# Attention queries in one DRAM tensor, head by head, instead of plain and rotary rows in two

## The chip, the cores and the metric

The kernel runs on one core of a Trainium2 chip, as one launch. The metric is the device time in microseconds (us). The core has TensorE (PE, matrix products into PSUM; its weight loads are shown as PEld), VectorE (DVE), ScalarE (ACT), GpSimd (POOL), and SyncE (SP), which in this kernel issues all DMA transfers, in the order of its own instruction stream. A transfer is carried out by up to sixteen DMA engines, which move its rows as packets and then report its completion.

## The reference, cut to what matters

One encoder layer over 1024 positions with 1024 channels: multi-head latent attention and a bidirectional RWKV-7 mixing side by side, merged through gates, then a gated feed-forward part. What the change touches is the query of the attention, 8 heads of 64 plain and 32 rotary dimensions:

```python
q = (c_q @ w_uq).reshape(B, S, MLA_HEADS, QK_NOPE + QK_ROPE)          # 8 heads x (64 + 32)
q_nope, q_rope = q[..., :QK_NOPE], q[..., QK_NOPE:]
q_nope = rms_norm(q_nope, qn_g)
q_rope = rope(rms_norm(q_rope, qr_g), cos[:, :, None, :], sin[:, :, None, :])
...
def rope(t, cos, sin):                       # pairs (i, i + 16)
    half = t.shape[-1] // 2
    t1, t2 = t[..., :half], t[..., half:]
    return jnp.concatenate([t1 * cos - t2 * sin, t2 * cos + t1 * sin], axis=-1)
...
s = q_nope . k_nope + q_rope . k_rope        # one rotary key for all heads
p = softmax(s / sqrt(96));  o = p @ v
```

A score is a sum over 96 dimensions, and the order of these does not matter as long as query and key have the same.

## The kernel before, in words

All values are float32. Products that need precision are made of three: each operand is split into a high part, rounded to TensorE's fast format (`hi`), and the rest (`lo`), and hi*hi, hi*lo and lo*hi are summed in PSUM. So queries and keys exist twice, as high and low part. Channels lie on the partitions, positions along the free dimension, mostly in halves of 512 (`HT`).

The stages in order of time: the norm of x and the first columns of the input projection (to about 100 us); the rest of the projection (`inproj`), between whose matmuls the up-projections of the latents are strewn (to about 320 us); from then the chunked RWKV scans, between whose steps "dense" work is put (`gates`, the last columns of the projection; `attention`, from about 580 to 1000 us; `branch0`); then the merge and the feed-forward part. PE's order is written out by hand: generators yield pieces of work with their cost in ns, and a planner with modelled times of the other engines picks which comes next. The other engines' orders are made by the scheduler of the language. SP works through its stream one by one: a transfer that waits for its source holds up those behind it.

The weights of a projection tile come in halves of 512 columns (`wload`, line 219): a transfer into one of two `wraw` buffers, a copy on ACT to `whi`, a subtraction on POOL (or DVE) to `wlo`, each with two buffers. The load after next is issued when the subtraction has freed its `wraw`.

The queries are made in two kinds of pieces.

- `mla_nope(j, True)` (line 596), j = 0 to 3, two halves each: 128 rows, which are the 64 plain dimensions of heads 2j and 2j + 1. They are lifted out of PSUM, normed, split into `hi` and `lo` (two buffers each, tags `hi` and `lo`), and each is written by one transfer to 128 rows of `d_qh` or `d_ql` (512 rows of 1024 positions).
- `mla_rope` (line 640), two halves: the tiles hold 16 rows of each of the 8 heads, one tile for the first and one for the second half of the rotation (`out` = 0, 1). They go to `d_qrh` or `d_qrl`, which have the shape [128, 2, 1024]: row 16 * head + frequency, and within it the half. So a head's 32 rotary rows are contiguous, in the order frequency, half.

The rotary key (`key_rope`, line 545) is written to every second row of `d_krh` and `d_krl` to match that order.

In attention, two sets `qh`, `kh` of high parts alternate over the heads, and there is one set `ql`, `kl` of low parts. Rows 0 to 63 are plain, 64 to 95 rotary, the rest padding: row 96 of `qh` takes the negative row maximum of the scores (from `mr`, line 1307), and the rows of the rotary key and the padding are loaded once (`pad`). `load_h(h + 1)` (lines 1272 to 1274) is issued early in head h, `load_l(h + 1, part)` (lines 1278 to 1280) in the second half of head h, when the columns are free. `maxima(h + 1)` runs `sc<-kh,qh` matmuls within head h, as soon as `qh` is there.

Of the kernel before, what the change touches and what calls it, by code (L numbers as in the profile page):

```python
# [10 lines left out]
F32 = mybir.dt.float32  # L11
# [9 lines left out]
T = 1024  # L21
# [66 lines left out]
def block_kernel(ctx: ExitStack, tc: tile.TileContext, a):  # L88
    nc = tc.nc
# [94 lines left out]
    def vc(name, i=0, rows=slice(0, 128)):  # L184
        o = VOFF[name] + i
        return vec[rows, o:o + 1]

    def dt(name, shape):
        return dr.tile(shape, F32, name=name)
# [2 lines left out]
    d_gl = [dt(f"d_gl{d}", [128, T]) for d in range(2)]  # L192
    d_rw = {q: dt(f"d_{q}", [128, NPAIR, T]) for q in ("r", "v", "kk", "x1", "x2", "s0", "s1", "bo")}
    d_obf = dt("d_obf", [128, NPAIR, T])
    d_qh, d_ql = (dt(f"d_q{x}", [512, T]) for x in "hl")
    d_qrh, d_qrl = (dt(f"d_qr{x}", [128, 2, T]) for x in "hl")
    d_kh, d_kl = (dt(f"d_k{x}", [512, T]) for x in "hl")
    d_krh = dt("d_krh", [64, T])
    d_krl = dt("d_krl", [64, T])
# [10 lines left out]
    def split(x, hi, lo, eng=None):  # L210
        S.copy(hi, x)
        (eng or G).tensor_tensor(out=lo, in0=x, in1=hi.bitcast(F32), op=sub)
# [3 lines left out]
    def wload(src, n, tag="w", bufs=None):  # L216
        wp = wpool[tag]
        raw = wp.tile([128, n], F32, tag=f"{tag}raw", name=f"{tag}raw")
        wpool["load"] = nc.sync.dma_start(raw, src)
        hi = wp.tile([128, n], R, tag=f"{tag}hi", name=f"{tag}hi", bufs=bufs)  # L220
        lo = wp.tile([128, n], R, tag=f"{tag}lo", name=f"{tag}lo", bufs=bufs)
        split(raw, hi, lo)
        return hi, lo
# [18 lines left out]
    def rsqrt_(out, ss, scale, bias):  # L242
        act(out, ss, AF.Ln, scale=scale, bias=bias)
        act(out, out, AF.Exp, scale=-0.5)
# [47 lines left out]
    def up1():  # L292
        return psm.tile([128, 512], F32, tag="up", name="up")

    def ss1():
        return psm.tile([128, 512], F32, tag="ss", name="ss")
# [79 lines left out]
    def tt(n, tag="tp", bufs=3, dtype=F32, w=T):  # L376
        return tp.tile([128, w], dtype, tag=tag, name=n, bufs=bufs)
# [44 lines left out]
    for dst, src in ((b64r, a["consts"][:, C_B64:]), (b16, a["b16"])):  # L422
        t = tt("bt", "sqb", 1, w=128)
# [46 lines left out]
    def parted(x, hi=None, lo=None):  # L470

        if hi is None:
            hi, lo = t5("ghi", "ghi", GB, R), t5("glo", "glo", GB, R)
        S.copy(hi, x)
        V.tensor_tensor(out=lo, in0=x, in1=hi.bitcast(F32), op=sub)
        return hi, lo
# [13 lines left out]
    def mul(ps, w, x, **kw):  # L490
        now[0] += 213 if w.dtype == R else 853
        return E.matmul(ps, w, x, **kw)
# [28 lines left out]
    def key_rope():  # L521
        kro = slice(64, 128)
        sq = tt("sqk")
        S.activation(sq[kro, :], l2[kro, :], AF.Square)
        yield "kr"
        rs = tt("rsk")
        for hs in HT:
            ss = ss1()
            mul(ss[kro], onef[kro, 0:64], sq[kro, hs], start=True, stop=True)
            rsqrt_(rs[kro, hs], ss[kro], 1.0 / 32, eps[kro])  # L530
        kr = tt("kr")
        V.scalar_tensor_tensor(out=kr[kro, :], in0=l2[kro, :], scalar=vc("gkr", 0, kro), in1=rs[kro, :], op0=mult, op1=mult)
        yield "kr2"
        A_, B_ = slice(64, 96), slice(96, 128)
        ka, kb = sq, rs
        V.tensor_tensor(out=ka[kro, :], in0=kr[kro, :], in1=cosT[kro, :], op=mult)
        V.scalar_tensor_tensor(out=kb[A_, :], in0=kr[B_, :], scalar=-1.0, in1=sinT[B_, :], op0=mult, op1=mult)
        V.tensor_tensor(out=kb[B_, :], in0=kr[A_, :], in1=sinT[A_, :], op=mult)
        V.tensor_tensor(out=ka[kro, :], in0=ka[kro, :], in1=kb[kro, :], op=add)
        for hs in HT:  # L540
            hi, lo = t5("hi", "hi", HB, R), t5("lo", "lo", HB, R)
            split(ka[kro, hs], hi[kro], lo[kro], V)
            for dst, src in ((d_krh, hi), (d_krl, lo)):
                for half in range(2):
                    nc.sync.dma_start(dst[half:32:2, hs], src[64 + 32 * half:80 + 32 * half, :].bitcast(F32))
        yield "kr3"

        z = tt("z")
        G.memset(z[0:64, :], 0.0)
        G.memset(z[32:33, :], 1.0)  # L550
        for dst, src in ((d_zero, z[0:32, :]), (d_krl[32:64, :], z[0:32, :]), (d_krh[32:64, :], z[32:64, :])):
            nc.sync.dma_start(dst, src)
        yield "kr3"

    def up(ps, wh, wl, xs, hs):
        n = len(xs)
        for k, (xh, xl) in enumerate(xs):
            ws = slice(k * 128, (k + 1) * 128)
            mul(ps, wh[:, ws], xh[:, hs], start=(k == 0), stop=False)
            mul(ps, wh[:, ws], xl[:, hs], start=False, stop=False)  # L560
            mul(ps, wl[:, ws], xh[:, hs], start=False, stop=(k == n - 1))
# [4 lines left out]
    def t5(n, tag="hs", bufs=HS_BUFS, dtype=F32):  # L566
        return tt(n, tag, bufs, dtype, w=512)

    def lift(ps):
        q, sq = t5("q"), t5("sqh")  # L570
        S.activation(sq, ps, AF.Square)
        V.tensor_copy(q, ps)
        return q, sq
# [6 lines left out]
    def mla_nope(j, isq):  # L580
        xs, src, g = ((cqx, "w_uq", gqs[:, 0:1]), (ckx, "w_uk", vc("gkn")))[0 if isq else 1]
        w = []

        def half(hs):
            if not w:
                w.extend(wload(a[src][j], 128 * len(xs), "s"))
            ps = up1()
            up(ps, *w, xs, hs)
            q, sq = lift(ps)
            pt = parted(sq)  # L590
            yield "up"
            hnorm(sq, pt, b64r, 64.0, [q], [g])
            hi, lo = t5("hi", "hi", HB, R), t5("lo", "lo", HB, R)
            split(q, hi, lo, V)
            for qd, kd, x in ((d_qh, d_kh, hi), (d_ql, d_kl, lo)):
                nc.sync.dma_start((qd if isq else kd)[j * 128:(j + 1) * 128, hs], x.bitcast(F32))
        return [half(hs) for hs in HT]

    def staged(todo):
# [14 lines left out]
    def mla_rope():  # L614
        ws = []

        def half(hs):
            two = []
            if not ws:
                ws.extend(wload(a["w_uq"][4 + i], 256, "s") for i in range(2))  # L620
            for i in range(2):
                ps = up1()
                up(ps, *ws[i], cqx, hs)
                two.append(lift(ps))
                if i == 0:
                    yield "rope"
            (q1, s1), (q2, s2) = two
            G.tensor_tensor(out=s1, in0=s1, in1=s2, op=add)
            pt = parted(s1)
            yield "up"  # L630
            hnorm(s1, pt, b16, 32.0, [q1, q2], [gqs[:, 1:2], gqs[:, 2:3]])
            for out, op in enumerate((sub, add)):
                hi, lo = t5("hi", "hi", HB, R), t5("lo", "lo", HB, R)
                t, o = t5("t", "ht", 2), t5("o", "ht", 2)
                V.tensor_tensor(out=o, in0=two[out][0], in1=cosT[:, hs], op=mult)
                G.tensor_tensor(out=t, in0=two[1 - out][0], in1=sinT[:, hs], op=mult)
                V.tensor_tensor(out=o, in0=o, in1=t, op=op)
                split(o, hi, lo, V)
                for dst, src in ((d_qrh, hi), (d_qrl, lo)):
                    nc.sync.dma_start(dst[:, out, hs], src.bitcast(F32))  # L640
                if out == 0:
                    yield "rope3"
        return [half(hs) for hs in HT]
# [602 lines left out]
    ql = kl = vh = vl = None  # L1246
# [23 lines left out]
    def load_h(h):  # L1270
        qh, kh = qk[h % 2]
        nc.sync.dma_start(kh[0:64, :].bitcast(F32), d_kh[64 * h:64 * h + 64])
        nc.sync.dma_start(qh[0:64, :].bitcast(F32), d_qh[64 * h:64 * h + 64])
        nc.sync.dma_start(qh[64:96, :].bitcast(F32), d_qrh[16 * h:16 * h + 16].rearrange("i f t -> (i f) t"))

    def load_l(h, part):
        hs = HT[part]
        nc.sync.dma_start(ql[0:64, hs].bitcast(F32), d_ql[64 * h:64 * h + 64, hs])
        nc.sync.dma_start(ql[64:96, hs].bitcast(F32), d_qrl[16 * h:16 * h + 16].rearrange("i f t -> (i f) t")[:, hs])
        nc.sync.dma_start(kl[0:64, hs].bitcast(F32), d_kl[64 * h:64 * h + 64, hs])  # L1280

    def load_v(p, part):
# [355 lines left out]
    for u in range(NU):  # L1638
        osb = None if u else wk.tile([128, 2, 512], F32, tag="osb", name="osb")
        ch = chain(u, qs_[u], lambda: osb)  # L1640
        for k in range(9):
            want = [(u, None, "t"), (u, 0, "bt")] if k == 0 else [(u, 1, "bt")] if k == 3 else []
            sparse = 0
            while True:
                t = max([ready] + [seen.get(x, math.inf) for x in want])
# [4 lines left out]
                x = prepare(not blocked and (thin or sparse and t < math.inf), not blocked and 0 < alone[0] < BATCH and due > -math.inf)  # L1650
# [10 lines left out]
            x = next(ch, None)  # L1661
# [370 lines left out]
    x = load_next(2)  # L2032
# [38 lines left out]
    for f in range(2, NF):  # L2071
# [31 lines left out]
        else:  # L2103
            x = load_next(f + 1)
# [160 lines left out]
```

## Time and profile before

| | |
|---|---|
| median of the runs shown | 1877.03 us (1876.88 to 1881.24) |
| the profiled execution | 1880.9 us; its span on the core 1879.1 us |
| granted TensorE clock, mean | 0.981 |
| busy: PE, PEld, DVE, ACT, POOL | 1811.9, 1466.9, 1234.6, 872.6, 576.1 us |
| DMA | 260777 packets, 211.01 MB, nearly all on the queue q1, which SP feeds |
| plain queries written | 16 transfers of 256 KB (`d_qh`, `d_ql`), 254.9 to 316.1 us |
| rotary queries written | 8 transfers of 256 KB (`d_qrh`, `d_qrl`), 225.7 to 254.4 us |
| queries read | 8 + 8 transfers for the high part, 16 + 16 for the low part, 313.1 to 962.9 us |

The page of the profile gives, in order: each engine's busy time; the span in forty slices, with a digit for the busy tenths of each engine, of the DMA engines and of the granted clock; the DMA queues; the chain of work that ended last; the costliest groups of instructions; the DMA issues by group. In a row such as `L596 SPq DMA_DIRECT2D d_qh<-hi`, L596 is the line of the kernel, SPq the sequencer that issues, and `out<-in` are the program's names. A time in brackets behind an instruction is how long its engine stood before it, and whose end released it. Many operations are recorded at a helper's line (L109, L124), so that they are told apart by their tiles.

### The profile page before, as it was taken

The numbers are of one execution on the slowest core, as the hardware profiler recorded it, in microseconds if no ns is written. First come the engines' busy times: TensorE is split into PE (matmuls) and PEld (weight loads), VectorE is DVE, ScalarE is ACT, GpSimd is POOL, SyncE is SP. The second block draws the span as 40 slices with busy tenths as digits, with TensorE's granted clock in tenths as the row PEclk, the third lists the DMA queues.
The fourth block names the chain that finished last, engine by engine and source line by source line (L and its number), as shares of the span: only waits on it lengthen the run. The fifth ranks groups of instructions, "written<-read, shape, count | busy, mean of one in ns | idle before, by whom it ended". The sixth has DMA issues, their size and how long they took to land.

```text
span 1879.1 us, 36769 instructions
## 1 busy us (share of the span) xinstructions
PE 1811.9 (96%) x14936; PEld 1466.9 (78%) x14936; DVE 1234.6 (66%) x1911; ACT 872.6 (46%) x1396; POOL 576.1 (31%) x522
## 2 busy tenths in 40 slices
PE   9979989999999999989999999989999999999998
PEld 7767867887888777767777778878888888888886
DVE  6967776535655777766573264788576666757667
ACT  6776675232333566655666444543232333323231
POOL 3412432322121333342433322336322222232221
PEclk9989999999999999998999999999999999999999
DMA  5146556754456445454435671111111111111112
GB/s 183 40 146 228 172 179 200 200 132 123 114 143 146 132 104 131 108 130 91 106 82 186 225 284 57 56 51 51 51 53 64 53 51 51 51 51 52 63 44 106
DMA packets 260777, 211.01 MB, mean 112 GB/s; under 512 B 127168, under 2 KB 204800, under 8 KB 260608
## 3 DMA queue, kind: packets, MB, share of 16 engines
q1 hardware_dynamic: 260608, 208.67, 37.3%
q8 instruction: 117, 1.92, 0.4%
q14 instruction: 52, 0.43, 0.1%
HBM read 145.00 MB, written 59.38 MB: 109 GB/s over the span
## 4 chain that ended last, share of the span: by engine, by line
PE 40%; DVE 5%; DMA 2%; ACT 2%; issue 1%; POOL 0%; SPq 0%; POOLq 0%; DVEq 0%; ACTq 0%
PE b L124 36%; PE st L124 2%; DVE x L109 1%; PE sc L124 1%; PE po L124 1%; DVE u L109 1%; DMA wraw<-w_merge 1%; DVE b L109 0%; PE ct L124 0%; DMA o<-d_oal 0%; DVE wlo L109 0%; DMA y<-d_y 0%; DVE wl L109 0%; DVE RR L109 0%; DVE tm L109 0%
## 5 line engine op out<-in xcount | busy, mean ns | idle before, releaser
L109 POOL TENSOR_TENSOR wlo<-wraw,whi 128x512 fp32r<-128x512 f32 x118 | 160.9, 1364 | 614.3 <-ACT whi L109 607.4
L124 PE MATMUL st<-hh,whi 128*128 128x512 f32 x408 | 169.4, 415 | 1.0 <-ACT hh L109 1.0
L124 PE MATMUL st<-hl,whi 128*128 128x512 f32 x408 | 162.4, 398 | 0.0
L109 DVE TENSOR_TENSOR x<-b,x 128x512 f32<-128x512 f32 x176 | 119.0, 686 | 53.4 <-PE b L124 53.4
L124 PE MATMUL st<-hh,wlo 128*128 128x512 f32 x408 | 139.3, 396 | 0.0
L109 POOL TENSOR_TENSOR pl<-pe,ph 128x512 fp32r<-128x512 f32 x62 | 80.5, 1300 | 167.2 <-ACT ph L109 156.4
L109 ACT CAST whi<-wraw 128x512 fp32r<-128x512 f32 x118 | 72.9, 618 | 119.1 <-issue 38.2
L109 DVE TENSOR_REDUCE mx<-sc 128x1 f32<-128x512 f32 x128 | 81.8, 682 | 30.6 <-PE sc L124 30.5
L124 PEld LDWEIGHTS st<-hh,whi 128*128 128x128 f32 x408 | 78.2, 192 | 20.1 <-ACT hh L109 1.7
L124 PEld LDWEIGHTS st<-hl,whi 128*128 128x128 f32 x408 | 78.3, 192 | 17.2 <-issue 1.2
L124 PEld LDWEIGHTS st<-hh,wlo 128*128 128x128 f32 x408 | 77.9, 191 | 17.4
L109 POOL TENSOR_TENSOR wl<-wraw,wh 128x512 fp32r<-128x512 f32 x22 | 28.9, 1312 | 173.1 <-ACT wh L109 163.3
L109 DVE TENSOR_TENSOR u<-b,p 128x512 f32<-128x512 f32 x42 | 29.0, 691 | 70.6 <-PE b L124 70.6
L124 PE MATMUL b<-sl,wh 128*128 128x512 f32 x176 | 68.8, 391 | 0.8 <-DVE sl L109 0.8
L124 PE MATMUL b<-sh,wh 128*128 128x512 f32 x176 | 68.8, 391 | 0.6 <-ACT sh L109 0.6
L124 PE MATMUL b<-sh,whi 128*128 128x512 f32 x176 | 68.6, 390 | 0.8 <-DVE x L109 0.8
L124 PE MATMUL b<-sh,wl 128*128 128x512 f32 x176 | 68.5, 389 | 0.0
L124 PE MATMUL b<-sl,whi 128*128 128x512 f32 x176 | 68.5, 389 | 0.0
L124 PE MATMUL b<-sh,wlo 128*128 128x512 f32 x176 | 68.5, 389 | 0.0
L109 DVE TENSOR_TENSOR pl<-st,ph 128x512 fp32r<-128x512 f32 x66 | 45.0, 684 | 28.1 <-ACT st L109 27.6
L109 ACT CAST whi<-s 128x512 fp32r<-128x512 f32 x33 | 20.5, 623 | 87.0 <-PE b L124 87.0
L124 PE MATMUL po<-ph,vhh 128*128 128x512 f32 x128 | 58.1, 454 | 1.8 <-ACT rc L109 1.8
(493 smaller groups left out, 5280.4 us busy)
## 6 DMA issues: line engine op xcount, KB each, us to landing
wraw<-w_in SPq DMA_DIRECT2D x64, 256.0 KB, 3.1
wraw<-w_fd SPq DMA_DIRECT2D x44, 256.0 KB, 3.4
AA<-w_fu SPq DMA_DIRECT2D x41, 256.0 KB, 2.9
A<-w_fg SPq DMA_DIRECT2D x41, 256.0 KB, 2.8
d_gate<-gt SPq DMA_DIRECT2D x32, 256.0 KB, 2.9
ld<-d_x SPq DMA_DIRECT2D x32, 256.0 KB, 4.3
d_s<-sg SPq DMA_DIRECT2D x8, 512.0 KB, 2.9
ld<-d_s SPq DMA_DIRECT2D x16, 256.0 KB, 4.1
```

Source lines behind the costliest of these rows:

```text
L109: return f(*args, **kw)
L124: return f(out, a, b, **kw)
```

## The change

`d_qh`, `d_ql`, `d_qrh` and `d_qrl` go. In their place is one tensor for the high and one for the low part, `d_q[0]` and `d_q[1]`, of shape [8, 96, 1024]: for each head its 64 plain rows, then its 32 rotary rows, the first half's 16 and then the second half's 16. A plain write goes to [2 heads, 64 rows, 512 positions], a rotary write to [8 heads, 16 rows, 512 positions]; the tiles in SBUF that they come from stay 128 x 512. A head's query is read by one transfer of 96 rows. The rotary key's rows are no longer interleaved, to match.

```diff
-    d_qh, d_ql = (dt(f"d_q{x}", [512, T]) for x in "hl")
-    d_qrh, d_qrl = (dt(f"d_qr{x}", [128, 2, T]) for x in "hl")
+    d_q = [dt(f"d_q{x}", [8, 96, T]) for x in "hl"]
...
-                    nc.sync.dma_start(dst[half:32:2, hs], src[64 + 32 * half:80 + 32 * half, :].bitcast(F32))
+                    nc.sync.dma_start(dst[16 * half:16 * half + 16, hs], src[64 + 32 * half:80 + 32 * half, :].bitcast(F32))
...
-            for qd, kd, x in ((d_qh, d_kh, hi), (d_ql, d_kl, lo)):
-                nc.sync.dma_start((qd if isq else kd)[j * 128:(j + 1) * 128, hs], x.bitcast(F32))
+            for qd, kd, x in ((d_q[0], d_kh, hi), (d_q[1], d_kl, lo)):
+                dst = qd[2 * j:2 * j + 2, 0:64, hs] if isq else kd[j * 128:(j + 1) * 128, hs]
+                nc.sync.dma_start(dst, x.bitcast(F32))
...
-                for dst, src in ((d_qrh, hi), (d_qrl, lo)):
-                    nc.sync.dma_start(dst[:, out, hs], src.bitcast(F32))
+                for dst, src in zip(d_q, (hi, lo)):
+                    nc.sync.dma_start(dst[:, 64 + 16 * out:80 + 16 * out, hs], src.bitcast(F32))
...
-        nc.sync.dma_start(qh[0:64, :].bitcast(F32), d_qh[64 * h:64 * h + 64])
-        nc.sync.dma_start(qh[64:96, :].bitcast(F32), d_qrh[16 * h:16 * h + 16].rearrange("i f t -> (i f) t"))
+        nc.sync.dma_start(qh[0:96, :].bitcast(F32), d_q[0][h])
...
-        nc.sync.dma_start(ql[0:64, hs].bitcast(F32), d_ql[64 * h:64 * h + 64, hs])
-        nc.sync.dma_start(ql[64:96, hs].bitcast(F32), d_qrl[16 * h:16 * h + 16].rearrange("i f t -> (i f) t")[:, hs])
+        nc.sync.dma_start(ql[0:96, hs].bitcast(F32), d_q[1][h][:, hs])
```

## The prediction

> **What bounds the kernel now.** I read the page's first two parts, then its chain, then the busy times by window, because the edit touches only the stage that writes the queries (255 to 316 us, below) and the attention that reads them (580 to 1000 us).
>
> ```profile
> span 1879.1 us, 36769 instructions
> PE 1811.9 (96%) x14936; PEld 1466.9 (78%) x14936; DVE 1234.6 (66%) x1911; ACT 872.6 (46%) x1396; POOL 576.1 (31%) x522
> PE   9979989999999999989999999989999999999998
> DMA  5146556754456445454435671111111111111112
> q1 hardware_dynamic: 260608, 208.67, 37.3%
> PE 40%; DVE 5%; DMA 2%; ACT 2%; issue 1%; POOL 0%; SPq 0%; POOLq 0%; DVEq 0%; ACTq 0%
> ```
>
> PE is busy for 96% and its order is written by hand, so what keeps PE waiting adds to the end nearly one for one, and what only shortens an engine that PE does not wait for adds nothing. Nearly all transfers go through one queue, q1, on sixteen DMA engines, 37.3% busy on average. The stage of the edit, by windows (busy of PE, PEld, DVE, ACT, POOL; granted clock; DMA share; GB/s):
>
> ```profile
> 225.00:255.00 30.00, 28.70 (x123) 22.41 (x121) 29.94 (x33) 18.56 (x28) 14.69 (x9) 1.00 0.44 152
> 255.00:325.00 70.00, 63.88 (x267) 51.08 (x268) 48.72 (x61) 46.62 (x67) 18.98 (x16) 0.98 0.59 195
> 325.00:345.00 20.00, 20.00 (x89) 16.54 (x89) 7.53 (x10) 6.08 (x9) 8.77 (x11) 1.00 0.91 260
> ```
>
> PE idles 6.1 of 70 us there; the DMA engines have 41% to spare on average, and right after it almost nothing.
>
> **The writes.** First and last of the sixteen plain-query writes, and weight loads issued between and after them on the same queue (start, duration of the issue):
>
> ```profile
> 254.86 0.36 SPq L596 DMA_DIRECT2D d_qh<-hi  x1
> 260.56 0.34 SPq L219 DMA_DIRECT2D wraw<-w_in  x1
> 316.11 0.75 SPq L596 DMA_DIRECT2D d_ql<-lo  x1
> 319.36 0.37 SPq L219 DMA_DIRECT2D wraw<-w_in  x1
> 328.27 0.38 SPq L219 DMA_DIRECT2D wraw<-w_in  x1
> ```
>
> Each carries a 128 x 512 tile, 256 KB, 128 rows of 2 KB. Bytes and rows stay. What changes is the nesting of the DRAM side: 128 rows in one run become 2 heads of 64 rows, and the rotary writes 8 heads of 16 rows. Whether that costs anything hangs on how many DMA engines a transfer is split over. Two windows of the DMA view show it, by counting packets: one around a 64-row load of the keys, one that holds the completions of two 128-row writes (issued at 694.92 and 696.27) and all of a transfer that has 8 rows of 512 B.
>
> ```profile
> DMA packets 81, 0.15 MB, mean 38 GB/s; under 512 B 16, under 2 KB 16, under 8 KB 80
> q1 hardware_dynamic: 80, 0.13, 10.9%
> kl<-d_kl SPq DMA_DIRECT2D x1, 128.0 KB
> ...
> 694.92 0.35 SPq L1342 DMA_DIRECT2D d_oah<-rc  x1
> DMA packets 226, 0.39 MB, mean 81 GB/s; under 512 B 40, under 2 KB 48, under 8 KB 224
> d_oal<-pv SPq DMA_DIRECT2D x1, 256.0 KB, 2.1
> qh<-mr SPq DMA_DIRECT2D x1, 4.0 KB
> ```
>
> The 64-row load leaves 80 packets, its 64 rows and 16 small ones: one completion from each of sixteen engines. In the second window 48 - 40 = 8 packets are the 8 rows of 512 B, and the 40 small ones are 16 + 16 for the two writes and 8 for this transfer, which thus ran on eight engines. It is the only transfer of the kernel with an outermost count below sixteen, and its engines are as many as that count. No row shows a transfer with a small outermost count and many rows inside; there the bounds are two engines (the outermost count decides) and sixteen (the rows in all decide). I take two, by the nearest row, the 8-row one.
>
> [...]
>
> What one engine moves in a time, from a stretch in which all were full (us, clock, share, GB/s):
>
> ```profile
> 8.00:11.00 3.00, 1.00 1.03 397
> ```
>
> 397 / 1.03 / 16 = 24.1 GB/s an engine. On sixteen engines a write takes 16 KB / 24.1 = 0.68 us of each; on two, 128 KB / 24.1 = 5.44 us of each of the two. Sixteen writes: 10.9 us before, 87.0 us after, on the two that carry them. These two also carry a sixteenth of every other transfer: 0.59 x 70 = 41.3 us in the window, less 10.9, makes 30.4. So they have 30.4 + 87.0 = 117 us to do in 70: **47 us too much**. The 20 us behind have 0.09 x 20 = 2 us free; 45 are left.
>
> Who waits. Every other load puts a sixteenth on those two engines and lands when they are done, so weight loads stand behind the writes. Against that stand leads (ACT's copies of weights, `whi`, and of queries, `hi`):
>
> ```profile
> 272.51 0.62 ACT L109 CAST hi<-q 128x512 fp32r<-128x512 f32 x1
> 280.01 0.62 ACT L109 CAST whi<-wraw 128x512 fp32r<-128x512 f32 x1 [1.00 <-PE po L124]
> 328.02 0.62 ACT L109 CAST whi<-wraw 128x512 fp32r<-128x512 f32 x1 [4.82 <-PE po L124]
> 333.46 0.62 ACT L109 CAST whi<-wraw 128x512 fp32r<-128x512 f32 x1 [0.92 <-PE po L124]
> ```
>
> With two `wraw` buffers the load of 260.56 feeds the copy of 280.01, 19 us later, that of 319.36 the copy of 328.02 (8.7 us), that of 328.27 the copy of 333.46 (5.2 us). `hi` and `lo` have two buffers each, so the third `hi` (272.51) must wait until the first write (254.86) has landed: 17.6 us of lead, and then ACT stands, with weight copies queued behind it. The lead swallows the backlog at first; by the last writes it is 5 to 9 us, of which a landing took about 3. I take 5 us absorbed (bounds 0 and 16, 19 less 3): **40 us** of PE waiting.
>
> Two corrections. After a PE stop of 2.4 us the matmuls ran slower for a while:
>
> ```profile
> 272.09 0.50 PE L124 MATMUL up<-cqh,shi 128*128 128x512 f32 x1 [2.38 <-ACT sg L109]
> 274.63 0.63 PE L124 MATMUL st<-hh,whi 128*128 128x512 f32 x1
> 275.06 0.63 PE L124 MATMUL st<-hl,whi 128*128 128x512 f32 x1
> 277.00 0.39 PE L124 MATMUL ss<-ghi,b64r 128*128 128x512 f32 x1
> 277.23 0.39 PE L124 MATMUL ss<-glo,b64r 128*128 128x512 f32 x1
> ```
>
> Steps of 0.43 us instead of 0.23, about eight of them: 1.6 us a stop. Two or three long stops: +4 (bounds 0 and 12). And part of the 6.1 us that PE idles now falls into the new waits: -4 (bounds 0 and -6). Together nothing.
>
> The rotary writes, eight on eight engines, take 1.36 instead of 0.68 us of each: 5.4 us more on half of the engines in a window with a share of 0.44. Nothing, hidden by 0.56 x 30 = 17 us of room; without that room the 5.4 us. The key's rotary writes only go to rows side by side instead of every second row: same 16 rows of 2 KB, nothing.
>
> **The reads.** One transfer instead of two, eight times for the high part and sixteen for the low. Bytes and rows stay; 24 issues go. Durations, and the only PE waits that touch them:
>
> ```profile
> L1273 SPq DMA_DIRECT2D qh<-d_qh x8: 587/595/1393, 313.1 to 916.2; - x8
> L1274 SPq DMA_DIRECT2D qh<-d_qrh x8: 581/582/936, 316.9 to 916.8; - x8
> L1279 SPq DMA_DIRECT2D ql<-d_qrl x16: 573/582/1962, 579.9 to 962.9; - x16
> PE sc L124 <- DMA qh<-d_qrh: 5.9, 3, 4.0
> ```
>
> 24 x 0.58 = 14 us of SP, which PE does not see but in those three waits (5.9 us in all, the longest 4.0). In front of each landing at most two issues go, one of `load_l` and one of `load_h`: 1.2 us. Three waits cut by at most 1.2 us give 3; I take **-2** (bounds 0 and -5.9), since the wait next in size on the same matmuls, DVE's row maxima, follows close.
>
> Sum: +40 - 2 = +38 on the profiled span, 1879.1 to 1917. The profiled execution took 1880.9 us, the median of the runs shown is 1877.03, so the forecast in those terms is 1877 + 38 = **1915 us**.
>
> **Rivals.** (1) Two engines, as above: the bounds of its terms (absorbed 0 to 16, slow clock up to 12, idle up to 6, reads up to 5.9) give 45 - 16 - 6 - 6 = +17 to 45 + 12 = +57: 1894 to 1934. For it: the 8 completions. (2) The writes spread over sixteen engines, since they have 128 rows; then only the reads are left, -2 and at best -5.9: 1871 to 1877, forecast 1875. This is the other side, and the case that the nesting of the DRAM side does nothing; it decides if a write of 2 x 64 rows leaves 16 completions. Against it: the same view shows 8. (3) Two engines, but other transfers aren't held up by them; then only the chain through `hi` and `lo` is left: a half costs 2 x 5.44 = 10.9 us, eight halves 87 us from 254.9 to 342, against a last issue at 316; the lead of 17.6 us and the last two halves, which nobody waits for (21.8), leave at most a few us, with ACT's stops some +5 to +15: 1887. Against it: all loads share q1. [...] (4) Besides two engines, waits between writes: all plain and rotary writes now go to one DRAM tensor with interleaved rows, and if a write is made to wait for the one before to land, SP stands 24 times for a landing (about 2 us beside the transfer itself, as d_oal's 2.1), with the weight loads behind it: 24 x 2 = 48 more, less what the backlog hides, half: 1940. Before, no such waits on d_qh or d_qrh appear although their halves interleave too.
>
> **How the numbers follow.** Chances: (1) 0.74, (2) 0.13, (3) 0.06, (4) 0.07. The time is that of (1). The range 1885 to 1946 holds all of (1), two thirds of (3) and over half of (4), 0.82 together; (2) lies outside. A change under 0.3% (5.6 us) can't be told from none. Faster: 0.03, the far end of (2) with a favourable shift of the order; same: 0.11, the rest of (2) and a little of (3); slower: 0.86.
>
> **What would show it.** The q1 count tells (1) from (2) apart: 24 loads less take 24 x 16 = 384 completions away, sixteen writes on two engines 16 x 14 = 224, eight on eight 8 x 8 = 64. So 260608 becomes 259936 by (1), 260224 by (2). By (1) the DMA share from 255 us on is lower and lasts longer, some 110 us instead of 70, while PE waits there for weight copies and ACT waits for `hi`; the stretch before 225 us is as now, and all behind it is only later. By (4) SP shows waits of L596 and L640 for DMAs. In attention, waits of `sc` for `qh` of about 4 us instead of 5.9. Wrong would be the forecast if the split follows the rows, or if the leads swallow more than 16 us.

## The result and the profile after

The changed kernel takes 1910.91 us (median; 1909.78 to 1912.08), the kernel before beside it 1876.95: ratio 1.017, 95% interval 1.0149 to 1.0191. Forecast were 1915 us and a range of 1885 to 1946.

Page of the changed kernel: span, PE and DMA digits in forty slices, and the two rows that count packets.

```profile
span 1908.1 us, 36728 instructions
PE 1811.7 (95%) x14936; PEld 1465.8 (77%) x14936; DVE 1237.4 (65%) x1911; ACT 872.8 (46%) x1396; POOL 576.2 (30%) x522
PE   9989978699999999998999999999999999999998
DMA  5147543564455645453434682111111111111112
DMA packets 260106, 211.02 MB, mean 111 GB/s; under 512 B 126496, under 2 KB 204128, under 8 KB 259936
q1 hardware_dynamic: 259936, 208.67, 36.5%
```

PE did the same 14936 matmuls in the same busy time, and all bytes are as before. The queue carries 259936 packets, the number forecast for two engines a plain write and eight a rotary write; with sixteen it would have been 260224.

Where the time went shows in the windows from the first plain write to the matmul at which the delay has stopped growing, first of the kernel before, then of the changed one. Both hold the same 320 matmuls, 66 DVE and 74 ACT instructions (POOL is four instructions behind in the second).

```profile
255.00:337.00 82.00, 75.88 (x320) 61.01 (x321) 53.95 (x66) 51.45 (x74) 23.44 (x22) 0.98 0.65 207
```

```profile
256.20:372.00 115.80, 84.36 (x320) 66.68 (x321) 53.66 (x66) 51.44 (x74) 19.03 (x18) 0.84 0.43 139
```

82.0 us became 115.8: +33.8, all of the difference between the medians (34.0). PE stands for 31.4 us instead of 6.1 (+25.3) and is busy 8.5 us longer at a mean granted clock of 0.84 instead of 0.98; DVE and ACT do the same in the same time. The DMA share *fell* from 0.65 to 0.43. A mean over sixteen engines hides that two of them are full, as the next views show.

The DMA view of the changed kernel in two stretches shows these two: 284 to 289 us, and 349 to 356 us around a weight load (digits: busy share of the sixteen in tenths; below them GB/s).

```profile
DMA  1111011110111011111011110101011111101111
GB/s 66 66 66 66 0 66 66 49 66 16 66 66 49 33 49 66 66 66 66 0 66 49 66 49 33 66 33 66 33 66 49 49 49 49 66 33 66 49 49 49
DMA packets 104, 0.26 MB, mean 52 GB/s; under 512 B 7, under 2 KB 7, under 8 KB 104
q1 hardware_dynamic: 104, 0.26, 13.1%
```

```profile
DMA  9999521111111111111111111111111112995799
GB/s 410 398 374 433 199 94 47 47 59 70 47 47 47 47 59 47 47 47 59 59 47 47 47 47 59 59 47 47 47 59 59 47 47 94 281 339 140 304 374 351
wraw<-w_in SPq DMA_DIRECT2D x1, 256.0 KB, 10.4
```

13.1% of sixteen engines is the time of two, and they move 52 GB/s. At that rate a write of 262 KB comes to 5.04 us. In the second stretch the queue does little else for five of seven microseconds (47 to 70 GB/s), and the weight load needs 10.4 us to land.

How this reaches PE: SP's issues and the two instructions behind the longest stop, from the timeline of the changed kernel (start, duration).

```profile
265.41 4.34 SPq L596 DMA_DIRECT2D d_ql<-lo  x1
...
284.61 4.89 SPq L694 DMA_DIRECT2D d_s<-sg  x1
...
349.02 5.12 SPq L1267 DMA_DIRECT2D kh<-d_krh  x1
...
355.68 0.38 SPq L218 DMA_DIRECT2D wraw<-w_in  x1
366.16 0.62 ACT L109 CAST whi<-wraw 128x512 fp32r<-128x512 f32 x1 [20.40 <-DMA wraw<-w_in]
366.82 0.80 PE L124 MATMUL st<-hh,whi 128*128 128x512 f32 x1 [14.33 <-ACT whi L109]
367.42 0.63 PE L124 MATMUL st<-hl,whi 128*128 128x512 f32 x1
367.85 0.63 PE L124 MATMUL st<-hh,whi 128*128 128x512 f32 x1
```

With the two engines behind, SP's issues themselves stand, up to 5.3 us each where they took 0.3 to 0.8 in this stage of the kernel before. The weight load of 355.68 comes late out of SP, lands 10.4 us later, ACT's copy has waited for 20.4 us and PE for 14.3; then PE steps 0.43 us a matmul.

That stop is not the whole of it. Three waits of PE are new in this stage, and together, at 25.5 us, they are the added standing (total, times, longest; before, PE waited 7.4 us in this stage, for other things):

```profile
PE st L124 <- ACT whi L109: 14.3, 1, 14.3
PE ss L124 <- ACT phi L109: 7.3, 1, 7.3
PE up L124 <- ACT at L109: 3.9, 1, 3.9
```

Only the first goes through a weight. Behind the other two are writes of two RWKV tiles, `at` and `kf`, which SP issued between the plain-query writes: ACT and DVE are to fill these tiles again and stand until the writes have landed.

```profile
ACT at L109 <- DMA d_x<-at: 4.4, 1, 4.4
DVE kf L109 <- DMA d_x<-kf: 5.7, 1, 5.7
```

SP's issues of the two `kf` writes, before and after:

```profile
296.15 1.09 SPq L704 DMA_DIRECT2D d_x<-kf  x2
307.64 5.63 SPq L704 DMA_DIRECT2D d_x<-kf  x2
```

### The profile page after: what moved, and what is told of

It reads as the page before. It is cut to its first block, busy times and chain, and to the rows that moved or that the text cites. A ratio compares the mean times of both kernels' runs of the same rounds, so it can differ in the third digit from the quotient of the medians.

```text
span 1908.1 us, 36728 instructions
## 1 busy us (share of the span) xinstructions
PE 1811.7 (95%) x14936; PEld 1465.8 (77%) x14936; DVE 1237.4 (65%) x1911; ACT 872.8 (46%) x1396; POOL 576.2 (30%) x522
## 2 busy tenths in 40 slices
DMA packets 260106, 211.02 MB, mean 111 GB/s; under 512 B 126496, under 2 KB 204128, under 8 KB 259936
## 3 DMA queue, kind: packets, MB, share of 16 engines
q1 hardware_dynamic: 259936, 208.67, 36.5%
## 4 chain that ended last, share of the span: by engine, by line
PE 41%; DVE 4%; ACT 2%; DMA 2%; issue 1%; POOL 0%; SPq 0%; ACTq 0%; DVEq 0%; POOLq 0%
PE b L124 36%; PE st L124 2%; DVE x L109 1%; PE po L124 1%; PE sc L124 1%; PE ct L124 1%; DVE u L109 1%; DMA wraw<-w_merge 1%; DVE b L109 0%; DMA y<-d_y 0%; DVE wlo L109 0%; DMA o<-d_oal 0%; DMA o<-d_obl 0%; ACT L109 0%; DVE wl L109 0%
## 5 line engine op out<-in xcount | busy, mean ns | idle before, releaser
L124 PE MATMUL st<-hh,whi 128*128 128x512 f32 x408 | 170.9, 419 | 16.5 <-ACT whi L109 14.3
L109 DVE SCALAR_TENSOR_TENSOR cv<-u,vec,cv 128x1023 f32<-128x1023 f32 x42 | 56.5, 1345 | 3.5 <-ACT cv L109 1.4
```

Source lines behind the costliest of these rows:

```text
L109: return f(*args, **kw)
L124: return f(out, a, b, **kw)
```

## The experiments

**The plain writes by head.** `e1_by_head`, and once more as `e11_by_head`, is the changed kernel with each plain write in two:

```diff
-                dst = qd[2 * j:2 * j + 2, 0:64, hs] if isq else kd[j * 128:(j + 1) * 128, hs]
-                nc.sync.dma_start(dst, x.bitcast(F32))
+                if isq:
+                    for i in range(2):
+                        nc.sync.dma_start(qd[2 * j + i, 0:64, hs], x[H[i], :].bitcast(F32))
+                else: ...
```

> The changed kernel, but each plain-query tile is written by two transfers of 64 rows, one for each head, so that the outermost count is 64 again. Theory A (the 2 x 64 nesting puts a write on two DMA engines, and these have more to do than the stage has time): the delay of 34 us goes, 1877 us within 4; queue q1 shows 260416 packets (259936, and 16 times 32 - 2 completions more). Theory B (the cost is in the reads, or in waits that come from one shared tensor): it stays near 1911. What is then left against the kernel before is the one read in place of two and the rotary writes on eight engines: 0 to -3 us.

Measured: ratio 0.998 to the kernel before (0.9964 to 0.9995).

```profile
span 1873.3 us, 36744 instructions
q1 hardware_dynamic: 260416, 208.67, 37.7%
255.00:325.00 70.00, 64.12 (x275) 51.44 (x276) 48.84 (x62) 46.20 (x67) 19.00 (x16) 1.00 0.68 205
```

The delay is gone, the count is as expected. One tensor for all queries, the order of the rotary rows and the single read cost nothing that can be told; theory B falls.

**The nesting alone.** `e2_nest2` is the kernel before with a spare row behind each head's 64:

```diff
-    d_qh, d_ql = (dt(f"d_q{x}", [512, T]) for x in "hl")
+    d_qh, d_ql = (dt(f"d_q{x}", [8, 65, T]) for x in "hl")
...
+                dst = qd[2 * j:2 * j + 2, 0:64, hs] if isq else kd[j * 128:(j + 1) * 128, hs]
```

> The kernel before, with one thing of the change alone: the plain-query tensors have a spare row behind each head's 64, so that a write goes to 2 heads x 64 rows that don't run on; all reads, the rotary part and the number of transfers are as before. Theory A: all of the delay, 1911 us within 6, and q1 at 260608 - 16 x 14 = 260384 packets. Theory B (reads, or one shared tensor): 1877.

Measured: 1910.11 us, ratio 1.0152 (1.0127 to 1.0177).

```profile
q1 hardware_dynamic: 260384, 208.67, 36.7%
PE st L124 <- ACT whi L109: 13.8, 1, 13.8
PE ss L124 <- ACT phi L109: 7.1, 1, 7.1
```

The same two long waits from a spare row alone, and a delay of 24 to 33 us by the interval, where that of the changed kernel is 28 to 36.

**Half as many.** `e3_hi_only`: the spare row for the high parts alone (`d_qh` of [8, 65, T], `d_ql` as before).

> The same nesting for the high parts only, so half as many slow writes. Theory A by its sum: the two engines have 30.4 + 8 x 0.68 + 8 x 5.44 = 79 us in 70, less 2 and 5 that room and lead take, so +2 us and with slow-clock stretches up to +9: 1877 to 1886. Theory C (each nested write costs its share of the 34 us, wherever it is): half, +17, 1894.

Measured: ratio 1.0022 (1.0002 to 1.0042), +4 us (0.4 to 7.9); theory C's +17 is far outside. Half the slow writes cost about an eighth of the 34 us, and by the interval at most a quarter, so the cost is not in proportion to the number of slow writes. It fits theory A, by which the question is whether the two engines have more to do than the stage lasts.

**Four engines.** `e4_nest4`: `d_q{x}` of [16, 33, T], a write to `qd[4 * j:4 * j + 4, 0:32, hs]`, a head's plain rows read as 32 and 32.

> The kernel before, with the plain writes nested 4 x 32 rows by a spare row behind each 32 (a head is then read as two transfers of 32 rows). Theory A: four engines, 2.72 us of each a write, 16 x 2.72 = 43.5 and 30.4 of other work make 74 us in 70, less 2 of room and 5 of lead: 0 to +4 us against the kernel before; q1 at 260608 - 16 x 12 + 24 x 16 = 260800 packets. Theory C (cost in proportion to what each write adds to its engines): (2.72 - 0.68) / (5.44 - 0.68) = 0.43 of 34, +15.

Measured: ratio 1.0027 (1.0009 to 1.0044), +5 us (1.7 to 8.3), just over theory A's +4, far from +15. The reads had changed too, so `e10_three_reads` is the kernel before with only these reads, 32 + 32 + 32 rows, and no nesting:

> The kernel before with the plain rows of a query read as two transfers of 32 rows, so three transfers a head and no nesting anywhere. It tells apart what made the 4 x 32 kernel 0.27% slower. If it was the number of reads (24 more, as one read fewer seemed to give 0.2%): +3 to +6 us here too. If it was four engines for the writes: 0 within 2 us here. q1 at 260608 + 384 = 260992.

Measured: ratio 1.0022 (1.0005 to 1.0039). In its trace PE's matmuls `sc` wait 8.1 us in all for `qh`, where they waited 5.9 before. So most or all of the 0.27% can be the reads, and the nesting of 4 x 32 rows costs nothing that this can tell. That it puts a write on four engines is theory A's estimate; no packet count here shows it.

**The rotary writes.** `e5_rope8`: the kernel before with `d_qr{x}` of [8, 33, T], written as 8 x 16 rows.

> The kernel before, with the rotary queries alone nested: 8 heads x 16 rows with a spare row, in the order half, frequency; reads still two transfers. Theory A: eight engines each, 5.4 us more on these, hidden by the room of that stretch: 1877 within 3, q1 at 260608 - 64 = 260544. Theory C (each nested write costs in proportion to what it adds to its engines): 8 x (1.36 - 0.68) against 16 x (5.44 - 0.68) that gave 34, so +2.4: 1879.

Measured: ratio 0.9991 (0.9975 to 1.0007); no cost. In time the interval is -4.7 to +1.3 us, so theory C's +2.4 lies outside it, though not by much.

```profile
q1 hardware_dynamic: 260544, 208.67, 37.5%
225.00:255.00 30.00, 28.73 (x124) 22.68 (x122) 29.94 (x33) 18.58 (x28) 14.70 (x9) 1.00 0.52 151
```

**A queue of its own.** `e6_act_queue`:

```diff
-                nc.sync.dma_start(dst, x.bitcast(F32))
+                (nc.scalar if isq else nc.sync).dma_start(dst, x.bitcast(F32))
```

> The changed kernel with the 2 x 64 writes of the plain queries issued from ACT, on a queue of their own, all other transfers on SP's queue as they are. Theory A1 (the loads behind them in the one queue, and SP's issues that stand, make the delay): the loads share the two engines but no longer stand behind the writes; what is left is the chain through the two hi and lo buffers, and ACT standing at its issues: +5 to +15 against the kernel before. Theory A2 (two engines with 117 us of work in 70 hold up everything, in whatever queue): +30 to +45.

Measured: 1911.87 us, ratio 1.0169 (1.0141 to 1.0197). Its page's queues, and three of ACT's issues:

```profile
q1 hardware_dynamic: 257856, 204.47, 36.4%
q10 hardware_dynamic: 2080, 4.19, 0.6%
```

```profile
261.68 1.56 ACTq L596 DMA_DIRECT2D d_qh<-hi  x1
...
266.55 4.96 ACTq L596 DMA_DIRECT2D d_ql<-lo  x1
...
291.19 5.55 ACTq L596 DMA_DIRECT2D d_ql<-lo  x1
```

Alone on queue q10, the sixteen writes leave 2080 packets, 130 each: 128 rows and two completions. That is the split, counted directly. The delay is about as large as in the changed kernel: theory A1's +5 to +15 did not come, and the time lies in theory A2's range. But the delay comes about in another way. The weight loads of 225 to 400 us, their issues (ns: shortest, median, longest) and landings, in the changed kernel:

```profile
L218 SPq DMA_DIRECT2D wraw<-w_in x19: 332/455/5117, 227.8 to 398.0; - x19
DMA to landing us min/median/max: 4.7/8.5/12.8
```

The same here, and the longest of SP's own waits for a landing:

```profile
L218 SPq DMA_DIRECT2D wraw<-w_in x19: 328/338/2283, 226.6 to 398.5; - x19
DMA to landing us min/median/max: 4.7/5.2/5.4
SPq L1268 <- DMA d_ql<-lo: 11.1, 1, 11.1
```

Off the queue of the slow writes, SP issues a weight load in 0.34 us at the median and 2.3 at most, where the changed kernel took up to 5.1. The loads whose landing the trace gives land in at most 5.4 us, where the changed kernel took up to 12.8 (and the kernel before up to 5.0). What was gained there was lost elsewhere: ACT stands at its issues, up to 5.55 us, SP stands 11.1 us until a slow write has landed, and PE's stops are more and shorter, the longest 6.8 us instead of 14.3. So order within the one queue does make loads late in the changed kernel, as theory A1 has it. Whether a second queue would help in time with an issuer that has nothing else to do, this run does not show.

**The number of reads.** `e9_two_reads` is the by-head kernel with 64 and 32 rows read apart again.

> The kernel with plain writes by head (two transfers of 64 rows), but each query read as 64 and 32 rows again, in two transfers. If the 0.2% that the by-head kernel stood below the kernel before comes from the single read: 0 against the kernel before. If it comes from elsewhere (order, clock): -2 to -6 us as there. q1 at 260416 + 24 x 16 = 260800.

Measured: ratio 0.9999 (0.9986 to 1.0012). And the by-head kernel again, beside the three-read kernel:

> The by-head kernel (two transfers of 64 rows a plain write, one read of 96 rows) beside the three-read kernel on one chip. If the number of reads counts: -2 to -5 us against the kernel before, and 6 to 9 under the three-read kernel. If the earlier 0.2% was scatter: 0 within 2.

Measured: ratio 0.9993 (0.9975 to 1.001), 1880.7 us against 1885.55 with three reads; these 4.9 us lie between what the two cases had forecast. One, two and three reads a head thus stand at 0.998 and 0.9993, at 0.9999, and at 1.0022. Three reads cost a little; a gain of one read over two is not shown, since the second time the interval takes in 1. The by-head kernel is the best version of the change found, not measurably slower than the kernel before and at most 0.4% faster.

## Why the prediction was right, step by step

- *Two engines, by the nearest row.* Right. The 8 completions of an 8-row transfer could not tell outermost count from rows, so this was a choice; the total of q1 (259936) and the 130 packets a write on q10 confirm it.
- *5.44 us a write on two engines.* Too dear: 52 GB/s over the two give 5.04. With it the sum reads 30.4 + 16 x 5.04 = 111 us in 70, 41 too much, less 2 of room and 5 of lead, 34; the stage took 33.8 more. This is the mis-sized term: 6 us. That the lead is 5 was chosen between 0 and 16, and no run measures it by itself, so that 34 and 33.8 agree so closely is luck.
- *Waiting +36 (40, less 4 that fall together), slow clock +4.* Measured +25.3 of standing and +8.5 of longer busy time. The clock term was half its size, the waiting too large by 11; their sum, 40, against 33.8. The step counted the slower matmuls as coming on top of the engines' surplus. The 34 of the sum above already match the whole delay, waiting and slow matmuls together, so these look to lie within it, not on top; this is worked out, no run shows it.
- *Who waits: weights and `hi`.* Right for the longest wait, ACT's `whi` for its `wraw`. Waits of ACT and DVE in the changed kernel, 255 to 380 us:

```profile
ACT whi L109 <- DMA wraw<-w_in: 29.4, 4, 20.4
ACT hi L109 <- DMA d_qh<-hi: 3.3, 1, 3.3
DVE lo L109 <- DMA d_ql<-lo: 7.7, 1, 7.7
```

  The two `hi` and the two `lo` buffers, on which rival (3) rested, make ACT and DVE stand 3.3 and 7.7 us, and no stop of PE goes back to either. Two things are missing from the working. SP's own issues stand, up to 5.1 us at a weight load, so that loads are late at their issue too, not only in the queue. And 11.2 of the 25.5 us of new waits come through the writes of `at` and `kf`, not through weights: other transfers between the plain-query writes were late as well. The surplus of the two engines priced this without saying where it would show.
- *Rotary writes hidden.* Right (`e5_rope8`, ratio 0.9991).
- *The reads, -2.* Wrong. `sc` waits for `qh` as long as before:

```profile
PE sc L124 <- DMA qh<-d_qh: 5.8, 3, 3.7
DMA to landing us min/median/max: 5.2/6.3/7.3
```

  The failed step is that fewer issues ahead bring the last landing forward. The one transfer of 96 rows (and those to `qh` beside it) needs 6.3 us to land where they needed 4.6 before, 1.7 us more, against the 0.6 us of an issue saved. In `e1_by_head` and `e11_by_head`, with the same single read, these waits make 5.0 and 5.3 us, so a gain near 1 us is possible and 2 is not seen.
- *Rival (2)* falls by the packet count, *(3)* by the loads and writes held up above (weight loads land in 8.5 us at the median, 3.5 before). *(4)*: no wait of L596 or L640 for a DMA appears among SP's in the stage.
- *Against the profile.* The profiled spans differ by 29.0, not 34. The attention, by the same 468 DVE instructions, gave some of it back, first before, then after:

```profile
604.00:958.00 354.00, 332.91 (x4746) 265.74 (x4740) 247.74 (x468) 212.47 (x389) 132.32 (x140) 0.95 0.46 113
```

```profile
638.70:986.20 347.50, 324.25 (x4748) 258.99 (x4742) 247.66 (x468) 212.47 (x389) 132.45 (x140) 0.98 0.47 115
```

  6.5 us less, with PE busy 8.7 less at a higher clock, so the gain is in the clock and not in the waits for reads; why the clock was higher is not shown. The execution profiled before, 1880.9 us, lay 3.9 over its median.

## What to carry to other kernels

How a transfer's rows were nested decided here how many DMA engines carried it: a write of 2 x 64 rows left two completions (130 packets each in `e6_act_queue`), one of 128 rows in one run or of one head's 64 left sixteen (q1 at 260608 before and 260416 in `e1_by_head`), and rotary writes of 8 x 16 rows took q1 to 260544, the count of eight. The runs varied the nesting on the DRAM side only. So write a block of two heads as two transfers, not as one of 2 x 64: ratio 0.998 to the kernel before, against 1.017. Read the split from a profile by counting small packets: the 64-row load left 16, a 2 x 64 write 2, and the two engines that this gives agree with the 13.1% of sixteen that were busy. And add up the work of the fullest engine against the length of the stage: the mean DMA share fell here from 0.65 to 0.43 while two engines held up everything. Counting the surplus only as far as it exceeds the room and the prefetch lead, 7 us by the author's estimate, fits the runs: half the slow writes cost about an eighth (9 - 7 = 2 us by theory A's sum, 4 measured), and all sixteen in the nesting of 4 x 32 rows cost nothing that could be told (1.0027, against 1.0022 with its reads alone).

## What the runs showed of the hardware that was not expected

The engine that issues the slow writes stands at its DMA issues, up to 5.3 us on SP in the changed kernel, for its other transfers too, where an issue took 0.3 to 0.8 in this stage of the kernel before, and up to 5.6 us on ACT in `e6_act_queue`. This looks to go with the queue that holds the slow writes and not with full engines alone, since in `e6_act_queue` SP had the same sixteen engines to feed and issued its weight loads in 0.34 us at the median. Moving the slow writes to a second queue let the weight loads land in 5.2 us at the median instead of 8.5, and gained no time, since ACT and SP then stood for the writes themselves, up to 5.6 and 11.1 us.
